# Fewer, wider tiles for the late modulation blocks in a hybrid decoder layer

## The chip, the cores and the metric

The kernel runs on one core of a Trainium2 chip. The metric is device time in microseconds (us), as the median of several executions. Before the change it is 1068.77 us, the median of 3 runs (1064.44 to 1072.26). The profile is of one further execution.

## What is computed

One layer of a decoder trunk works on 576 token rows: 512 of a prompt and 64 of eight samples. A condition vector `c` per prompt or sample (nine in all) is turned into six modulation vectors of 1024 each. Cut to what matters here, the reference is:

```
mod = silu(c) @ w_ada + b_ada                      # (9, 6144)
sh1, sc1, g1, sh2, sc2, g2 = split(mod, 6)
u = x * (1 + sc1) + sh1
z = u @ w_in                                       # pool, q, f, i, out gate, gate A, gate B
merged = sigmoid(z_ga) * (y_pool @ w_a) + sigmoid(z_gb) * (y_hgrn @ w_b)
x = layer_norm(ALPHA * x + g1 * (merged @ w_out))
h = x * (1 + sc2) + sh2
x = layer_norm(ALPHA * x + g2 * ((silu(h @ w_gate) * (h @ w_up)) @ w_down))
```

`w_ada` is 1024 by 6144, all of it float32: 24 MB. The first two of the six vectors (`sc1`, `sh1`) are needed at the start. The other four, 16 MB of weights, are needed only after the mixers, and the kernel computes them late, between the matmuls of the last gates. That late part is what the change is about.

## The kernel before, in words

The work is one program for five engines in these stages: the early modulation and `u`; `u @ w_in` with the two mixers, head by head; the eight gate pairs (`z_ga`, `z_gb`, 128 channels of each at a time); `y_pool @ w_a`; `y_hgrn @ w_b`; `merged @ w_out` with the first norm; the feed-forward; `w_down` with the second norm.

Large products are done by `fast` (line 210) as seven products of halves instead of eight. One product is twelve matmuls of 288 columns (`mm_q`, line 203, the matmuls have line 207), since each float32 operand is split in a high and a low part that are multiplied as hi*hi, hi*lo and lo*hi. `fast_w` (line 178) loads the two raw weight tiles of a product (512 KB each, three buffers `raw`, SyncE's queue) and makes the sums and splits of their quarters on POOL, ACT and DVE. `fast_u` (line 743) makes the weights of the next product ready and then runs the present one. `gate(m)` (line 786) is one such product for gate pair `m`. Its results go to the two tiles `SG[m]` (`sga`, `sgb`), first by an ACT copy (line 222), then by DVE additions (line 220). The seven products of a gate share four PSUM banks in turn.

`ada(blk)` (line 320) computes 256 columns of the modulation for the nine condition vectors. Its weights come as two tiles of four contraction blocks by 256 columns, 512 KB each with 1 KB of contiguous memory per row (`ada_load`, line 242, issue line 247). Each tile is multiplied by four float32 matmuls (line 328), one for each contraction block. They use 32 columns of the PE array each and write to different partitions of one PSUM bank (`tile_position`), so the four run side by side. I call these four matmuls a **batch**. Each float32 matmul shows as two instructions in the trace, so a batch is 8 instructions there. After two batches DVE copies the bank to `adaev` (line 332). For the two vectors that are wanted by channel (`SC2`, `SH2`), two small matmuls of nine columns (line 338, four instructions in the trace) add up the four partial sums and turn them, and DVE writes them to `mod` (line 340). For the two gates (`G1`, `G2`) the tile is stored in DRAM (`gada`, line 335), to be read and spread over the rows much later (`gate_bc`, line 889).

The sixteen late blocks are called in the loop over the gates (lines 802 to 805): three before each of the gates 2 to 5, two before 6 and 7. The pool `adap` holds three `ada` tiles and two `adaev` tiles. A scheduler in the compiler mixes the instructions of the blocks and the gates on each engine. Each engine, and SyncE's queue of loads, then runs its own instructions strictly in the order that is fixed when the program is built. A load that waits for a buffer holds back the loads behind it.

Two later places matter. `SG` tiles for gates 2 to 7 are taken at once (line 797) and stay until the product with `w_b` is merged. In the `w_out` stage (from line 990) SyncE's queue brings the eight `w_out` tiles (line 121), the rows of `x` for the residual (line 1000) and the first feed-forward weights (line 116), and DVE splits the weights (line 108) between its work for the norm (lines 926 to 948).

Of the kernel before, what the change touches and what calls it, by code (L numbers as in the profile page):

```python
# [9 lines left out]
ALU = mybir.AluOpType  # L10
PSUM = bass.MemoryType.PSUM

P = 128
D = 1024
KT = D // P
# [18 lines left out]
SH1, SC1, G1, SH2, SC2, G2 = 0, 8, 16, 24, 32, 40  # L34
# [3 lines left out]
C_ID, C_MP, C_MS, C_SEL, C_SP, C_SS, C_BM, C_RC, C_END = 0, 128, 256, 320, 330, 458, 522, 526, 552  # L38
# [27 lines left out]
def bcast(ap, n):  # L66

    return bass.AP(ap.tensor, ap.offset, list(ap.ap) + [[0, n]])


def trunk(tc, consts, x_prompt, x_sample, state_pool, state_hgrn, c_prompt, c_sample,
# [4 lines left out]
    pe, act, dve, pool, sp = nc.tensor, nc.scalar, nc.vector, nc.gpsimd, nc.sync  # L76
    pl = Pools(tc)
    t_ = pl.t
# [10 lines left out]
    s0, _s0 = pl.open("s0", "right")  # L89
# [3 lines left out]
    cst = t_(cp, [P, C_END], "cst")  # L93
# [3 lines left out]
    R_LB, R_NW, R_PS, R_BA, R_LG, R_LO, R_END = 0, 16, 24, 28, 76, 84, 92  # L97
# [35 lines left out]
    def prefetch(n):  # L133
        while len(ready) < n and seq:
            ready.append(load_w(seq.pop(0)))
# [31 lines left out]
    def split(hi, lo, src, eng=dve):  # L167
        act.copy(out=hi, in_=src)  # L168
        return eng.tensor_tensor(out=lo, in0=src, in1=hi.bitcast(F32), op=ALU.subtract)  # L169
# [72 lines left out]
    def ada_load(pl_, blk):  # L242

        raws = []
        for j in range(2):
            raw = t_(pl_, [P, 4, 256], "ada", bufs=8 if pl_ is s0 else 3)
            ada_last[0] = sp.dma_start(out=raw, in_=w_ada[0][j * 512:(j + 1) * 512, blk * 256:(blk + 1) * 256]
                         .rearrange("(k p) n -> p k n", p=P))
            raws.append(raw)
        return raws  # L250
# [56 lines left out]
    cpad = t_(ym, [P, KT, 32], "cpad")  # L307
    pool.memset(cpad, 0.0)
    pc = t_(psA, [P, 512], "t", bufs=2)
    for kt in range(KT):  # L310
        pe.transpose(out=pc[:, kt * 16:kt * 16 + 9], in_=sc_[:, kt * P:(kt + 1) * P], identity=ident[:9, :9])
    dve.tensor_copy(out=cpad[:, :, 0:9],
                    in_=pc[:, :P].rearrange("p (k c) -> p k c", c=16)[:, :, 0:9])

    mod = t_(cp, [P, 48, 9], "mod")

    dr, _dr = pl.open("gada", space=bass.MemoryType.DRAM)
    gada = {G1: t_(dr, [P, 4, 256], "gada1"), G2: t_(dr, [P, 4, 256], "gada2")}

    def ada(blk, pl_, psp, tag, raw=None):  # L320

        if raw is None:
            raw = ada_load(pl_, blk)
        ps = t_(psp, [P, 512], tag, bufs=2 if tag == "t" else 4)
        for st in range(2):
            for g in range(4):
                kt = st * 4 + g
                pe.matmul(out=ps[32 * g:32 * g + 32, :256], lhsT=cpad[:, kt, :], rhs=raw[st][:, g, :],  # L328
                          start=st == 0, stop=st == 1, tile_position=(0, 32 * g))
        m = blk * 2  # L330
        ev = t_(pl_, [P, 256], "adaev", bufs=2)
        dve.tensor_copy(out=ev, in_=ps[:, :256])
        if G1 <= m < SH2 or m >= G2:
            base = G1 if m < SH2 else G2
            sp.dma_start(out=gada[base][:, (m - base) // 2], in_=ev)
            return
        for j in range(2):
            pe.matmul(out=ps[:, 256 + 16 * j:256 + 16 * j + 9], lhsT=ev[:, j * P:(j + 1) * P],
                      rhs=cst[:, C_SEL:C_SEL + 9], start=True, stop=True)
        dve.tensor_tensor(out=mod[:, m:m + 2], in0=ps[:, 256:288].rearrange("p (j c) -> p j c", j=2)[:, :, 0:9],  # L340
                          in1=bcast(prow[:, R_BA + m:R_BA + m + 2], 9), op=ALU.add)

    prow = t_(cp, [P, R_END], "prow")
# [27 lines left out]
    for b in range(4):  # L371
        for kt in (2 * b, 2 * b + 1):
# [6 lines left out]
                              in1=bcast(sc[:, 1:9], LS), op=ALU.mult)  # L379
# [19 lines left out]
    def st_():  # L399
        return t_(psB, [P, 512], "s", bufs=4)  # L400
# [78 lines left out]
    psB, _psB = pl.open("psB", "right", space=PSUM)  # L479
# [146 lines left out]
    def vg():  # L626
        return t_(hp, [P, T], "v"), t_(hp, [P, T], "g", bufs=2)
# [95 lines left out]
    def hg4(h):  # L723
# [3 lines left out]
        for i in range(4):  # L727
# [5 lines left out]
        dve.scalar_tensor_tensor(out=YB[:, h, TP:T], in0=px[:, :TS], scalar=nw, in1=s["g"][:, TP:T],  # L733
                                 op0=ALU.mult, op1=ALU.mult)

    ada_todo = [SC2 // 2 + b for b in range(4)] + [SH2 // 2 + b for b in range(4)] + \
               [G1 // 2 + b for b in range(4)] + [G2 // 2 + b for b in range(4)]

    pairs = iter([(win(a + h), win(b + h)) for h in range(1, NH) for a, b in ((M_F, M_Q), (M_I, M_OG))] +
                 [(win(M_GA + m), win(M_GB + m)) for m in range(KT)])  # L740
# [10 lines left out]
    v, g = vg()  # L751
# [13 lines left out]
    psF, _psF = pl.open("psF", "left", space=PSUM)  # L765
    for h in range(1, NH):
# [4 lines left out]
        v, g = vg()  # L771
# [8 lines left out]
    def sg_open(n):  # L780
        p, cm = pl.open(f"sg{n}", "right")
        m0 = len(SG)
        SG.extend([[t_(p, [P, T], f"sg{x}{m}") for x in "ba"][::-1] for m in reversed(range(m0, m0 + n))][::-1])
        return cm

    def gate(m, mid=None):
        fast_u(*SG[m], mid)
        for x in SG[m]:
            act.activation(out=x, in_=x, func=AF.Sigmoid)

    _sga = sg_open(2)
# [2 lines left out]
    gate(1, lambda: hg3(NH - 1))  # L794
    hg4(NH - 1)
    pl.close(_hp)
    _sgb = sg_open(KT - 2)
    yah, _yah = pl.open("yahl", "right")
    YAH = t_(yah, [P, 4, T], "yah", F32R)
    YAL = t_(yah, [P, 4, T], "yal", F32R)  # L800
    adap, _adap = pl.open("ada", "right")
    for m in range(2, KT):
        for i in range(3 if m < 6 else 2):
            ada(ada_todo.pop(0), adap, psB, "s")
        gate(m)
        if m < 6:
            split(YAH[:, m - 2], YAL[:, m - 2], YA[:, m - 2])
        if m == KT - 1:
            seq += [("c", w_a[0], m, 4) for m in range(KT)]
            prefetch(2)  # L810
    pl.close(_adap)
    pl.close(_wu)
    pl.close(_tu)
    pl.close(_U)
# [4 lines left out]
    yt, _yt = pl.open("yt", "right")  # L819
    wy, _wy = pl.open("wy", "right")  # L820
# [17 lines left out]
    psF, _psF = pl.open("psF", "left", space=PSUM)  # L838
# [10 lines left out]
    for m in range(0, KT, 2):  # L849
# [9 lines left out]
        for i in range(2):  # L859
            a, b = SG[m + i]  # L860
            pool.tensor_tensor(out=b, in0=o[i], in1=b, op=ALU.mult)
            dve.tensor_tensor(out=a, in0=a, in1=b, op=ALU.add)
            split_act(MM[:, m + i], a)
    for c in (_wy, _yt, _yah, _sgb, _sga, _psF, _psB):
        pl.close(c)


# [13 lines left out]
    def bk():  # L881
        return t_(psC, [P, 512], "b", bufs=8)
# [6 lines left out]
    def gate_bc(pool_, mb):  # L889

        ga = t_(pool_, [P, D], "ga")
        act.dma_start(out=ga, in_=gada[mb].rearrange("p a b -> p (a b)"))
        act.dma_start(out=ga[R_BIAS:R_BIAS + 1], in_=b_ada[0:1, mb * P:mb * P + D])
        gp = t_(pool_, [P, D], "gp")
        gs = t_(pool_, [TS, D], "gs")
        for o, n, c in ((gp, P, C_SP), (gs, TS, C_SS)):
            for j in range(2):
                ps = bk()
                pe.matmul(out=ps[:n], lhsT=cst[:, c:c + n], rhs=ga[:, j * 512:(j + 1) * 512], start=True, stop=True)
                act.copy(out=o[:, j * 512:(j + 1) * 512], in_=ps[:n])  # L900
        return gp, gs
# [88 lines left out]
    ps = [bk() for i in range(5)]  # L990
    st = [t_(lp, [P, 2, 6], f"st{i}") for i in range(5)]
# [16 lines left out]
    for n, i in enumerate(order):  # L1008
        ps = bk()
# [36 lines left out]
    raw = load_raw(gate_up(1)[1])  # L1046
# [49 lines left out]
    g = [gemm_2(w) for w in w3[:2]]  # L1096
    swiglu(0, 1, *g)
    g = [gemm_2(w) for w in w3[2:]]
# [46 lines left out]
    st = [t_(dp, [P, 2, 6], f"st{i}") for i in range(5)]  # L1145
# [32 lines left out]
    ps = [bk() for i in range(5)]  # L1178
    for k in range(FT // 2):
# [3 lines left out]
        if 4 <= k < 9:  # L1183
            i = order[k - 4]
            n = P if i < 4 else TS
# [7 lines left out]
    ps = {i: bk() for i in order[:-1]}  # L1193
# [36 lines left out]
    for i in order[:-1]:  # L1230
        n = P if i < 4 else TS
# [7 lines left out]
    i = order[-1]  # L1239
    stl = t_(dp, [P, 3, 6], "stl")  # L1240
    act.copy(out=stl[:, 0], in_=st[i][:, 0])
    for h in range(2):
        for k in range(NL):
            down_part(FT // 2 - NL + k, *last[k], pe_[h], h)
        c = slice(512 + h * 256, 768 + h * 256)
# [59 lines left out]
```

## Time and profile before

| what | value |
|---|---|
| median of 3 runs | 1068.77 us (1064.44 to 1072.26) |
| the profiled execution, own time | 1066.02 us |
| its span, first to last instruction | 1063.9 us |
| around the span | 2.1 us |
| PE busy, share of the span | 984.7 us, 93% |
| VectorE (DVE) busy | 853.2 us, 80% |
| ScalarE (ACT) busy | 478.7 us, 45% |
| GpSimd (POOL) busy | 413.2 us, 39% |
| moved by DMA | 120.00 MB, mean 113 GB/s |
| mean granted TensorE clock | 0.977 of full speed |

PE is the matmul unit, PEld its weight loads. A busy time counts pipelined matmuls from their start to their modelled end, so consecutive matmuls overlap in it. Where a rate matters, the distance from one start to the next is read. In the chain of waits the profile follows the last instruction back through what released each step. Idle time before an instruction stands in brackets with what ended it.

### The profile page before, as it was taken

The page shows a single profiled execution, that of the slowest core. Times are in us where ns is not written, and L with a number is a line of the kernel's source. Part 1 is how long each engine was busy: PE and PEld are TensorE (multiplying, and loading weights), DVE is VectorE, ACT ScalarE, POOL GpSimd, SP SyncE. Part 2 cuts the span into 40 slices and gives each one's busy share as a digit, 9 for nine tenths or more (in the row PEclk, how much of TensorE's full clock was granted, in tenths as well). Part 3 has the DMA queues.
Part 4 walks back from the last instruction along what each step waited for, and adds up shares of the span by engine and source line. Part 5 has one row for each costly group of instructions (what it writes and reads, how often), then busy time and mean ns, then how long its engine had stood idle before and what let it go on. Part 6 is the DMA issues. An engine that isn't in the chain of part 4 may idle for free.

```text
span 1063.9 us, 17728 instructions
## 1 busy us (share of the span) xinstructions
PE 984.7 (93%) x6807; PEld 898.2 (84%) x6807; DVE 853.2 (80%) x1450; ACT 478.7 (45%) x861; POOL 413.2 (39%) x297
## 2 busy tenths in 40 slices
PE   5995889989999899999898998999999999999993
PEld 3885879989999897789897677999999999788882
DVE  3479998989989966436989498999999999957428
ACT  4342456665566464234333336444444434643312
POOL 1168675757666646365374011112212220000004
PEclk9997999999989999999999999999999999999997
DMA  9932142223323228893224810232332333432202
GB/s 258 293 90 66 41 121 81 83 83 102 100 72 93 87 78 255 274 282 101 89 71 130 256 40 21 60 93 87 99 95 85 99 91 110 139 119 80 80 20 89
DMA packets 170120, 120.00 MB, mean 113 GB/s; under 512 B 4286, under 2 KB 158938, under 8 KB 170028
## 3 DMA queue, kind: packets, MB, share of 16 engines
q1 hardware_dynamic: 168367, 114.25, 35.9%
q10 hardware_dynamic: 1668, 4.63, 1.3%
q8 instruction: 53, 0.87, 0.3%
q14 instruction: 32, 0.25, 0.1%
HBM read 110.57 MB, written 8.40 MB: 112 GB/s over the span
## 4 chain that ended last, share of the span: by engine, by line
PE 64%; DVE 21%; DMA 6%; issue 4%; POOL 2%; ACT 2%; SPq 0%; DVEq 0%; ACTq 0%; POOLq 0%
PE b L207 23%; PE f L207 16%; PE z L150 4%; DVE wlo L169 4%; PE b L1158 4%; PE b L1157 3%; PE b L1156 3%; DMA ada<-in_w_ada 2%; DMA raw<-in_w_in 2%; DMA raw<-in_w_up 2%; DVE tmp L581 1%; PE s L328 1%; DVE S L682 1%; PE b L1162 1%; PE b L1161 1%
## 5 line engine op out<-in xcount | busy, mean ns | idle before, releaser
L168 ACT CAST whi<-st 128x512 fp32r<-128x512 f32 x184 | 109.0, 618 | 105.4 <-POOL st L193 30.4
L169 DVE TENSOR_TENSOR wlo<-st,whi 128x512 fp32r<-128x512 f32 x140 | 127.7, 931 | 6.5 <-ACT whi L168 5.8
L187 POOL TENSOR_TENSOR st<-raw 128x512 f32<-128x512 f32 x36 | 56.8, 1578 | 134.9 <-DVE wlo L169 59.0
L207 PE MATMUL f<-uh,whi 128*128 128x288 f32 x352 | 106.7, 303 | 2.7 <-DVE tmp L220 1.6
L207 PE MATMUL f<-ul,whi 128*128 128x288 f32 x352 | 106.2, 302 | 0.0
L207 PE MATMUL f<-uh,wlo 128*128 128x288 f32 x352 | 105.8, 301 | 0.0
L108 DVE TENSOR_TENSOR wlo<-raw,whi 128x1024 fp32r<-128x1024 f32 (+1 forms) x46 | 55.1, 1197 | 34.8 <-ACT whi L107 34.5
L168 ACT CAST whi<-raw 128x1024 fp32r<-128x1024 f32 x46 | 48.3, 1049 | 76.5 <-PE f L207 32.6
L188 POOL TENSOR_TENSOR st<-st,raw 128x512 f32<-128x512 f32 x46 | 62.4, 1358 | 51.3 <-issue 49.6
L107 ACT CAST whi<-raw 128x1024 fp32r<-128x1024 f32 (+1 forms) x49 | 47.9, 978 | 63.0 <-PE b L1158 20.0
L1158 PE MATMUL b<-whi,hl 128*128 128x512 f32 (+1 forms) x198 | 72.6, 367 | 0.0
L1157 PE MATMUL b<-whi,hl 128*128 128x512 f32 (+1 forms) x198 | 72.5, 366 | 0.0
L207 PEld LDWEIGHTS f<-uh,whi 128*128 128x128 f32 x352 | 66.8, 190 | 6.6 <-DVE tmp L220 1.9
L1156 PE MATMUL b<-wlo,hl 128*128 128x512 f32 (+1 forms) x198 | 72.4, 365 | 0.0
L193 POOL TENSOR_TENSOR st<-raw,st 128x512 f32<-128x512 f32 x26 | 40.8, 1568 | 75.6 <-DVE wlo L169 71.3
L207 PEld LDWEIGHTS f<-ul,whi 128*128 128x128 f32 x352 | 66.8, 190 | 2.8 <-issue 2.5
L207 PEld LDWEIGHTS f<-uh,wlo 128*128 128x128 f32 x352 | 66.9, 190 | 2.2 <-issue 1.6
L1225 POOL TENSOR_TENSOR x<-x,lg 128x640 f32<-128x640 f32 (+2 forms) x4 | 5.9, 1465 | 160.0 <-ACT x L1216 160.0
L169 DVE TENSOR_TENSOR wlo<-raw,whi 128x1024 fp32r<-128x1024 f32 x46 | 65.0, 1413 | 3.2 <-ACT whi L168 3.1
L169 POOL TENSOR_TENSOR wlo<-st,whi 128x512 fp32r<-128x512 f32 x44 | 60.3, 1389 | 10.8 <-ACT whi L168 6.5
L207 PE MATMUL b<-bh,whi 128*128 128x288 f32 x184 | 54.5, 296 | 2.1 <-ACT bh L168 2.1
L207 PE MATMUL b<-bh,wlo 128*128 128x288 f32 x184 | 55.2, 300 | 0.0
(459 smaller groups left out, 3359.9 us busy)
## 6 DMA issues: line engine op xcount, KB each, us to landing
raw<-in_w_in SPq DMA_DIRECT2D x52, 512.0 KB
ada<-in_w_ada SPq DMA_DIRECT2D x48, 512.0 KB
raw<-in_w_gate SPq DMA_DIRECT2D x22, 512.0 KB
raw<-in_w_down SPq DMA_DIRECT2D x22, 512.0 KB
raw<-in_w_up SPq DMA_DIRECT2D x12, 512.0 KB
rawu<-in_w_up SPq DMA_DIRECT2D x10, 512.0 KB
s<-in_state_hgrn SPq DMA_DIRECT2D x8, 512.0 KB
out<-sn SPq DMA_DIRECT2D x8, 512.0 KB
```

The source lines that it names most:

```text
L107: act.copy(out=hi[:, :n], in_=raw[:, :n])
L108: eng.tensor_tensor(out=lo[:, :n], in0=raw[:, :n], in1=hi[:, :n].bitcast(F32), op=ALU.subtract)
L150: mm = pe.matmul(out=ps[:, GA0 + c0:GA0 + c1], lhsT=a[:, kt * P:(kt + 1) * P], rhs=x[:, kt, c0:c1], start=first and i == 0, stop=last and ...
L168: act.copy(out=hi, in_=src)
L169: return eng.tensor_tensor(out=lo, in0=src, in1=hi.bitcast(F32), op=ALU.subtract)
L187: pool.tensor_tensor(out=s1, in0=a21, in1=a22, op=ALU.add)
L188: pool.tensor_tensor(out=s2, in0=s1, in1=a11, op=ALU.subtract)
L193: eng.tensor_tensor(out=s4, in0=a12, in1=s2, op=ALU.subtract)
L207: pe.matmul(out=ps, lhsT=x[:, k * P:(k + 1) * P], rhs=y[:, k], start=first and k + i == 0, stop=last and k == 3 and i == 2)
L1156: pe.matmul(out=o, lhsT=xh, rhs=lo, start=first, stop=False)
L1157: pe.matmul(out=o, lhsT=xl, rhs=hi, start=False, stop=False)
L1158: return pe.matmul(out=o, lhsT=xh, rhs=hi, start=False, stop=last)
```

## The change

The late modulation gets its own function, `ada_late(m)`. It does 512 columns at a time from tiles of four contraction blocks by 512 columns, 1 MB each with 2 KB of contiguous memory per row. So there are 8 late blocks with two batches of 512 columns each (16 batches), where there were 16 blocks with two batches of 256 (32 batches). The copy to `adaev` takes 512 columns, and four small matmuls follow for `SC2` and `SH2`, into another PSUM bank. There are two `ada` buffers of 1 MB instead of three of 512 KB, and one `adaev` tile of 2 KB per partition instead of two of 1 KB. Gates 2 to 4 are each preceded by two late blocks, gates 5 and 6 by one, and gate 7 by none. The tiles of gate 7 are no longer taken with those of gates 2 to 6. They are taken when the pool of the modulation is closed, in memory that it held. The DRAM tiles `gada` lose their middle dimension. The early modulation keeps its size.

```diff
@@ ada_load
-            raw = t_(pl_, [P, 4, 256], "ada", bufs=8 if pl_ is s0 else 3)
+            raw = t_(pl_, [P, 4, 256], "ada", bufs=8)
@@
-    gada = {G1: t_(dr, [P, 4, 256], "gada1"), G2: t_(dr, [P, 4, 256], "gada2")}
+    gada = {G1: t_(dr, [P, D], "gada1"), G2: t_(dr, [P, D], "gada2")}
@@ ada
-        if G1 <= m < SH2 or m >= G2:
-            base = G1 if m < SH2 else G2
-            sp.dma_start(out=gada[base][:, (m - base) // 2], in_=ev)
-            return
@@
-    ada_todo = [SC2 // 2 + b for b in range(4)] + [SH2 // 2 + b for b in range(4)] + \
-               [G1 // 2 + b for b in range(4)] + [G2 // 2 + b for b in range(4)]
+    def ada_late(m, pl_):
+
+        ps = st_()
+        for st in range(2):
+            raw = t_(pl_, [P, 4, 512], "ada", bufs=2)
+            sp.dma_start(out=raw, in_=w_ada[0][st * 512:(st + 1) * 512, m * P:m * P + 512].rearrange("(k p) n -> p k n", p=P))
+            for g in range(4):
+                pe.matmul(out=ps[32 * g:32 * g + 32], lhsT=cpad[:, st * 4 + g, :], rhs=raw[:, g, :],
+                          start=st == 0, stop=st == 1, tile_position=(0, 32 * g))
+        ev = t_(pl_, [P, 512], "adaev")
+        dve.tensor_copy(out=ev, in_=ps)
+        if G1 <= m < SH2 or m >= G2:
+            base = G1 if m < SH2 else G2
+            sp.dma_start(out=gada[base][:, (m - base) * P:(m - base) * P + 512], in_=ev)
+            return
+        px = st_()
+        for j in range(4):
+            pe.matmul(out=px[:, 16 * j:16 * j + 9], lhsT=ev[:, j * P:(j + 1) * P],
+                      rhs=cst[:, C_SEL:C_SEL + 9], start=True, stop=True)
+        dve.tensor_tensor(out=mod[:, m:m + 4], in0=px[:, :64].rearrange("p (j c) -> p j c", j=4)[:, :, 0:9],
+                          in1=bcast(prow[:, R_BA + m:R_BA + m + 4], 9), op=ALU.add)
+
+    ada_todo = [SC2, SC2 + 4, SH2, SH2 + 4, G1, G1 + 4, G2, G2 + 4]
@@
-    _sgb = sg_open(KT - 2)
+    _sgb = sg_open(KT - 3)
...
     for m in range(2, KT):
-        for i in range(3 if m < 6 else 2):
-            ada(ada_todo.pop(0), adap, psB, "s")
+        for i in range(2 if m < 5 else 1 if m < KT - 1 else 0):
+            ada_late(ada_todo.pop(0), adap)
+        if m == KT - 1:
+            pl.close(_adap)
+            _sgc = sg_open(1)
         gate(m)
...
-    pl.close(_adap)
```

In the program as built, the matmuls of the late modulation stand between those of the gates on **PE**. Before, in gate 3 (`f_` a bank of the gate, `s_` one of the modulation; L328 a batch or half of one, L338 the small matmuls, L207 the gate):

```order
L328 MATMUL s_4688<-ada_4684,cpad_196 32x256 x2
L338 MATMUL s_4670<-cst_73,adaev_4679 128x9 x2
L328 MATMUL s_4688<-ada_4684,cpad_196 32x256 x2
L207 MATMUL f_4794<-t1l_833,whi_4537 128x288
L207 MATMUL f_4794<-t1h_832,wlo_4538 128x288
L207 MATMUL f_4808<-uh_81,whi_4539 128x288
L328 MATMUL s_4688<-ada_4686,cpad_196 32x256 x4
```

With the change, also in gate 3 (L739 a batch, L749 the small matmuls):

```order
L749 MATMUL s_4511<-cst_73,adaev_4509 128x9 x4
L739 MATMUL s_4652<-ada_4653,cpad_196 32x512 x4
L207 MATMUL f_4796<-uh_81,wlo_4526 128x288
L207 MATMUL f_4811<-t4h_836,hq_4545 128x288
L207 MATMUL f_4811<-t4l_837,hq_4545 128x288
L207 MATMUL f_4811<-t4h_836,lq_4546 128x288
```

The batches are twice as wide and half as many. Between two matmuls of the gates PE turns to the modulation at 30 places before and at 17 with the change, and no batch is cut in two any more. In the first gates a batch still follows after some 9 to 34 matmuls of a gate.

On **SyncE's queue** the loads of the modulation (`ada`) stand between those of the next gates (`raw`). Before, from the start of gate 2:

```order
L174 DMA raw_4533<-in_w_in 128x8x128
L247 DMA ada_4477<-in_w_ada 128x4x256
L247 DMA ada_4479<-in_w_ada 128x4x256
L247 DMA ada_4495<-in_w_ada 128x4x256
L174 DMA raw_4720<-in_w_in 128x8x128
L247 DMA ada_4497<-in_w_ada 128x4x256
L247 DMA ada_4513<-in_w_ada 128x4x256
L247 DMA ada_4515<-in_w_ada 128x4x256
L174 DMA raw_4722<-in_w_in 128x8x128
```

With the change, from the same place:

```order
L174 DMA raw_4519<-in_w_in 128x8x128
L737 DMA ada_4476<-in_w_ada 128x4x512
L737 DMA ada_4482<-in_w_ada 128x4x512
L174 DMA raw_4694<-in_w_in 128x8x128
L737 DMA ada_4497<-in_w_ada 128x4x512
L174 DMA raw_4696<-in_w_in 128x8x128
L737 DMA ada_4503<-in_w_ada 128x4x512
L174 DMA raw_4861<-in_w_in 128x8x128
```

Two loads of 1 MB lie ahead at the start instead of three of 512 KB, and the fourth of 1 MB stands behind the second `raw` load of gate 4.

The scheduler also moved something that the diff does not touch: on **SyncE's queue** in the `w_out` stage. Before (`x1` the rows for the residual):

```order
L174 DMA rawu_1298_7272<-in_w_up 128x8x128
L121 DMA raw_1198_6523<-in_w_out 128x2x512
L121 DMA raw_1201_6530<-in_w_out 128x2x512
L121 DMA raw_1204_6537<-in_w_out 128x2x512
L1000 DMA x1_1166_6431<-in_x_prompt 128x1024 x4
L1000 DMA x1_1166_6431<-in_x_sample 64x1024
L116 DMA raw_1207_6629<-in_w_gate 128x8x128
```

With the change:

```order
L174 DMA rawu_1270_7152<-in_w_up 128x8x128
L121 DMA raw_1170_6403<-in_w_out 128x2x512
L1019 DMA x1_1138_6311<-in_x_prompt 128x1024 x4
L1019 DMA x1_1138_6311<-in_x_sample 64x1024
L121 DMA raw_1173_6410<-in_w_out 128x2x512
L121 DMA raw_1176_6417<-in_w_out 128x2x512
L116 DMA raw_1179_6509<-in_w_gate 128x8x128
```

The five `x` loads now stand ahead of the last two `w_out` loads.

## Rows read from the trace of the kernel before

**Rows 1.** The page: busy time, share of the span and instructions.

```profile
PE 984.7 (93%) x6807; PEld 898.2 (84%) x6807; DVE 853.2 (80%) x1450; ACT 478.7 (45%) x861; POOL 413.2 (39%) x297
```

**Rows 2.** Busy us (instructions) of PE, PEld, DVE, ACT, POOL; clock; DMA share, GB/s.

```profile
407.40:497.00 89.60, 88.40 (x747) 71.11 (x746) 42.36 (x85) 30.70 (x49) 44.43 (x34) 1.00 0.81 249
497.00:510.00 13.00, 9.85 (x73) 9.41 (x72) 12.82 (x7) 6.91 (x9) 9.95 (x3) 1.00 0.14 40
...
596.00:600.00 4.00, 4.00 (x17) 2.81 (x17) 1.23 (x1) 2.49 (x4) 0.00 (x0) 1.00 1.04 403
```

**Rows 3.** The chain of waits, gates 2 to 7: start us, us, what.

```profile
407.54 0.57 PE s L328 x8
408.11 1.13 PE f L207 x7
...
415.88 6.21 DMA ada<-in_w_ada
...
443.20 5.49 DMA ada<-in_w_ada
...
454.63 1.43 PE s L328 x24
...
465.36 4.33 PE f L207 x31
469.70 1.00 PE s L328 x16
```

**Rows 4.** The timeline of PE: start, us, line, names, tile shape; idle before.

```profile
407.11 0.29 PE L207 MATMUL f<-t1l,whi 128*128 128x288 f32 x1
407.24 0.29 PE L207 MATMUL f<-t1h,wlo 128*128 128x288 f32 x1
...
427.32 0.63 PE L328 MATMUL s<-ada,cpad 128*32 128x256 f32 x4
427.88 0.61 PE L338 MATMUL s<-cst,adaev 128*128 128x9 f32 x4
428.42 0.62 PE L328 MATMUL s<-ada,cpad 128*32 128x256 f32 x4
428.98 0.40 PE L207 MATMUL f<-t1l,whi 128*128 128x288 f32 x1
...
592.86 2.96 PE L899 MATMUL b<-ga,cst 128*128 128x512 f32 x6 [0.60 <-DMA ga<-in_b_ada]
```

**Rows 5.** Groups of PE's instructions, 407.4 to 497: count, busy us, mean ns, idle before.

```profile
L328 PE MATMUL s<-ada,cpad 128*32 128x256 f32 x256 | 20.6, 389 | 1.2 <-DMA ada<-in_w_ada 1.1
...
L338 PE MATMUL s<-cst,adaev 128*128 128x9 f32 x32 | 4.6, 252 | 0.0
```

**Rows 6.** PE and PEld of line 207 alone in that stretch.

```profile
407.40:497.00 89.60, 68.36 (x458) 61.47 (x456) 1.00 0.81 249
```

**Rows 7.** Who SyncE's queue waited for, 407 to 497: total us, times, longest.

```profile
SPq L247 <- PE s L328: 17.4, 20, 1.9
```

**Rows 8.** Timelines of SyncE's queue and of DVE in the `w_out` stage.

```profile
591.23 2.75 SPq L1000 DMA_DIRECT2D x<-in_x_prompt  x4
...
595.29 3.76 SPq L116 DMA_DIRECT2D raw<-in_w_up  x1
...
607.30 1.22 DVE L108 TENSOR_TENSOR wlo<-raw,whi 128x1024 fp32r<-128x1024 f32 x1 [8.46 <-ACT whi L107]
609.11 1.22 DVE L108 TENSOR_TENSOR wlo<-raw,whi 128x1024 fp32r<-128x1024 f32 x1 [0.58 <-ACT whi L107]
610.33 1.37 DVE L926 TENSOR_TENSOR r<-b,gp 128x512 f32<-128x512 f32 x2
```

**Rows 9.** The chain of waits and PE's timeline, behind those loads.

```profile
595.29 12.64 DMA raw<-in_w_up
...
629.03 1.09 PE L967 MATMUL b<-cst,x 128*128 128x128 f32 x8 [1.37 <-DVE x L948]
```

More of the change, by code (lines that the diff above doesn't have):

```diff
@@ L323, in ada @@
             raw = ada_load(pl_, blk)
-        ps = t_(psp, [P, 512], tag, bufs=2 if tag == "t" else 4)
+        ps = t_(psp, [P, 512], tag, bufs=2)
         for st in range(2):
@@ L863, in trunk @@
             split_act(MM[:, m + i], a)
-    for c in (_wy, _yt, _yah, _sgb, _sga, _psF, _psB):
+    for c in (_wy, _yt, _sgc, _yah, _sgb, _sga, _psF, _psB):
         pl.close(c)
@@ L891, in gate_bc @@
         ga = t_(pool_, [P, D], "ga")
-        act.dma_start(out=ga, in_=gada[mb].rearrange("p a b -> p (a b)"))
+        act.dma_start(out=ga, in_=gada[mb])
         act.dma_start(out=ga[R_BIAS:R_BIAS + 1], in_=b_ada[0:1, mb * P:mb * P + D])
```

## Prediction

> **What bounds the kernel now.** I read the page first. PE is busy for 93% of the span [rows 1], so most changes must take work or waits from PE to show. Then the busy times by stretch, for the gates 2 to 7, in which the late modulation lies. From 407.4 to 497 us PE is busy 88.4 of 89.6 us, while DVE, ACT and POOL have half their time free or more and the DMA engines stand at 0.81 [rows 2]. So the stretch is PE's, with loads as the next limit. Right behind it, 497 to 510, DVE is busy 12.82 of 13 us and PE waits [rows 2]. That stretch starts from the results of gate 7 and should move with them as a whole. Then the chain of waits, which alternates between the gates (line 207) and the batches (line 328), with two loads of `ada` in it [rows 3]. Last, the order as built, for what the scheduler made of the change.
>
> A busy PE is not PE at its best, so I split these 89.6 us by starts. In the chain, 31 gate matmuls take 4.33 us and 7 take 1.13 us [rows 3]. The difference is 24 matmuls in 3.20 us, 0.133 us each, as their starts show (407.11 to 407.24 [rows 4]). Seven at that rate are 0.93, so resuming after a batch costs 0.20. The stretch holds 456 gate matmuls by the program (the trace has 458 records [rows 6]): 60.7 us. The other 28.9 us are the modulation and what surrounds it.
>
> **The change, part by part.**
>
> *Batches.* One batch alone takes 0.57 us on the chain, two in a row 1.00, three 1.43 [rows 3]. A further batch of 256 columns therefore streams in 0.43, and turning to the modulation costs 0.14. With the 0.20 for resuming, a visit costs 0.34. Before: 32 batches x 0.43 = 13.8; 30 visits x 0.34 = 10.2; waits of PE for `ada` 1.2 [rows 5]; what is left of 28.9 is 3.7 for the eight pairs of small matmuls, 0.46 a pair (one inside a batch took 0.54, from 427.88 to 428.42 [rows 4]).
>
> With the change: 16 batches of twice the columns stream the same 13.8. There are 17 visits: 5.8. Each of the four sets of small matmuls now has four: it costs between 0.46 (if a set costs what a pair did) and 0.92 (two pairs). They stay separate matmuls with their own weight loads, so I take 0.80: 3.2. Sum 22.8, which is 6.1 under 28.9 if nothing waits.
>
> The trace has no batch of 512 columns. From below it is 0.43 x 2 with one start; from above, two separate batches, 2 x 0.57 = 1.14, which adds 16 x 0.14 = 2.2. The nearest row with 512 float32 columns is line 899: six instructions, three matmuls, in 2.96 us, so 0.99 each with all starts and stops [rows 4]. Four side by side that cost 1.00 fit that, so I take the lower value.
>
> *Loads.* This is the part that can take the gain back. With two buffers, a load of 1 MB is issued when the batch two before it is done, and must land before PE comes to its own batch. Between the second and the twelfth batch in the new order stand 230 gate matmuls (30.6 us), ten batches (10.0), four sets of small ones (3.2) and resumes (about 2.8): 46.6 us, or 9.3 for two batches. Less one batch of 1.0, a load has 8.3 us. A load of 512 KB on the chain took 5.49 and 6.21 us to land [rows 3]. Another 512 KB adds 1.3 us at the 403 GB/s of 596 to 600 and 2.1 at this stretch's mean of 249 [rows 2]: 6.8 to 8.3 us. That just fits, but the batches are not evenly spaced. Where only 9 gate matmuls lie between two batches the later load is late, and one load stands behind a `raw` load that waits for POOL. I bound the waits from 0 to 3 us. SyncE's queue, which waited for PE's batches 20 times before [rows 7], still does, so they do not vanish. I take 1.6, somewhat above the 1.2 of now. The stretch is then 6.1 - 1.6 = **4.5 us** shorter.
>
> The Trainium skill, "DMA: Bandwidth & Descriptors", section "Bandwidth", puts a core's reads from HBM at about 358 GB/s at most, which speaks against any gain from the longer rows. Here a stretch of 4 us moved 403 GB/s [rows 2], so the trace does not agree. At 358 the added 512 KB would take an estimated 1.5 us instead of 1.3, and the sum would stay.
>
> *DVE, ACT, POOL.* Half as many copies of twice the width, half as many additions to `mod`, half as many stores: nothing on the path, since DVE is idle for half of the stretch [rows 2]. One `adaev` tile instead of two: a copy waits until the small matmuls or the store of the block before have read it. Blocks are over 7 us apart, and a store is smaller than the loads that landed in 5.49 to 6.21 [rows 3].
>
> *Gate 7's tiles.* ACT's first copy of gate 7 now waits until the last `adaev` is stored. The last batch stands after the first matmul of gate 6's last product. Behind it come 23 gate matmuls, 3.1 us, to the end of gate 7's first product. PE can go on for three more products in the other banks, 3 x 12 x 0.133 = 4.8 us. So the store has 7.9 us. Copy and landing need about 0.8 + 6.2 = 7.0, with the slowest load as the bound. I cost it at nothing. If it took longer, each us over 7.9 would stop PE. Queued behind the copy on ACT are only splits for `w_a`, which have the same cover.
>
> *The moved `x` loads.* In the `w_out` stage the five `x` loads (issued from 591.23 before [rows 8]) now stand ahead of the last two `w_out` loads. These have buffers to wait for, so the `x` loads use a gap, and 2.25 MB no longer lie in front of the `w_gate` and `w_up` loads. Before, a `w_up` load issued at 595.29 took 12.64 us and stands on the chain [rows 9]. The two splits behind it sit on DVE at 607.30 and 609.11, each 1.22, directly ahead of the norm's first work at 610.33 [rows 8], and PE later waits 1.37 for that DVE work [rows 9]. Landing earlier takes the second split (1.22) from that path. The gain lies between 0 and the 1.37 of that wait, plus a 0.60 wait at line 899 [rows 4] that the new order fills with other matmuls. A later landing of the last two `w_out` tiles could cost as much, but they are wanted only after the first half. I take **1.1**, near the split, less a little for two norm steps that move behind others on DVE.
>
> *Sum.* 4.5 + 1.1 = 5.6 us. The profiled execution took 1066.02 us (span 1063.9 and 2.1 around it) and would take 1060.4. It lies 2.7 under the median of the runs shown, 1068.77, from which the same sum gives 1063.2. I forecast 1063.0 as a median.
>
> **Rivals.**
>
> *A. The wide batches save little.* Each batch of 512 columns costs 1.14 (2.2 back), the small sets cost 0.92 (0.5 back), waits reach 3 (1.4 back) and the moved loads bring nothing (1.1). 5.6 - 5.2 leaves 0.4: 1068.4. For it: no row shows such a batch beside gates. Against it: the clean 0.43 steps for batches in a row.
>
> *B. Slower: the two buffers make PE wait in every batch.* Two loads are never far ahead, and for ten batches each pair takes landing plus 1.0. At a landing of 9.7 us a pair takes 10.7 where 9.3 stand in the sum. That is 1.4 x 5 = 7.0 lost, 1.6 of it already counted, so the 5.6 is gone. At 12 us it is 13 - 9.3 = 3.7 x 5 = 18.5: 16.9 beyond the sum, 11.3 over now, 1080. For it: `raw` loads stand between in the same queue, and another load took 12.64 us when the queue was full [rows 9]. Against it: 5.49 to 6.21 in this very stretch [rows 3].
>
> *C. Much more is won.* No waits in the stretch (1.6 more), sets at 0.46 (1.4), the whole 1.37 and 0.60 at the moved loads (0.9), and DVE's full stretch from 497 on starts with its `w_a` weights ready, so that part of PE's 3.15 us there goes (say 2): 5.6 + 5.9 = 11.5, 1057. For it: every one of these is a wait that rows show. Against it: all must come at once.
>
> *D. The change doesn't do what it says.* Gate 7's tiles come so late that PE stands still: at a landing of 10 us the store needs 10.8, 2.9 over its cover, and the gain shrinks to 2.7: 1066. It needs a store slower than any load of the stretch.
>
> **How the numbers follow.** Forecast 0.60, A 0.15, B 0.09, C 0.10, D 0.06. A measurement of this kernel can tell about 1% (10.7 us) from no change. Faster by more than that comes from C and the luckiest of the forecast: 0.12. Slower by more comes from B's far end: 0.07. The rest, 0.81, is within 1%. The likeliest case's own terms reach from 3 to 9 us of gain, 1060 to 1066, and three runs of the kernel before lie 8 us apart. The range 1055 to 1071 holds all but part of B and the ends of C.
>
> **What would show it.** On PE: batches of line 739 alone at about 1.00 us from start to the next gate matmul; resumes of 0.20; sets of line 749 at 0.8; waits for `ada` of 1 to 3 us in all, most of them in gates 3 and 4; the time from the start of gate 2 to the first `w_a` matmul shorter by 4 to 5. On ACT: the copy to `sga7` not ended by a store, or with PE not idle. In the `w_out` stage: the `w_gate` and `w_up` loads landed well before the first half ends, and the norm's first step not behind a split. Wrong would be loads of 1 MB that land later than 8.3 us as a rule, batches near 1.14, or a PE wait in gate 7.

## The result and the profile after

| | before | after |
|---|---|---|
| median | 1066.40 us of 15 runs (1062.43 to 1072.26) | 1058.51 us of 15 runs (1054.87 to 1065.18) |
| ratio | | 0.9928, 95% interval 0.9906 to 0.9949 |
| the profiled execution, and its span | 1066.02 and 1063.9 us | 1061.09 and 1059.3 us |

The changed kernel is 0.7% faster. The interval is a gain of 5.4 to 10.0 us; the working of the prediction came to 5.6.

First the stage of gates 2 to 7, by the windows: busy us (and instructions) of PE, PEld, DVE, ACT and POOL, then clock, DMA share and GB/s. Before, it ran from 407.40 to 497 [rows 2].

```profile
407.40:492.00 84.60, 83.15 (x619) 67.30 (x618) 40.09 (x73) 30.92 (x49) 44.30 (x34) 1.00 0.80 260
492.00:505.00 13.00, 9.88 (x74) 9.44 (x72) 12.78 (x8) 6.93 (x9) 9.96 (x3) 1.00 0.14 42
```

The stage is 5 us shorter, PE is still busy for all but 1.45 us of it, and the DVE stretch behind it only moved. The chain of waits shows what PE does there (start, us, what), to be held against [rows 3].

```profile
413.37 3.50 PE f L207 x25
416.87 0.79 PE s L749 x8
417.66 1.00 PE s L739 x8
418.65 3.50 PE f L207 x25
422.15 1.05 PE s L739 x8
...
448.83 1.04 PE s L739 x8
449.89 8.54 DMA ada<-in_w_ada
458.47 1.11 PE s L739 x8
459.60 8.93 DMA ada<-in_w_ada
468.57 1.06 PE s L739 x8
```

A batch of 512 columns takes 0.99 to 1.11 us, mostly 1.00. A set of four small matmuls takes 0.79. 25 gate matmuls in 3.50 us are 25 x 0.133 = 3.32 and a resume of 0.18. Two loads of 1 MB stand on the chain, and the groups of PE in this stretch say what they cost.

```profile
L739 PE MATMUL s<-ada,cpad 128*32 128x512 f32 x128 | 17.0, 604 | 1.4 <-DMA ada<-in_w_ada 1.3
...
L749 PE MATMUL s<-cst,adaev 128*128 128x9 f32 x32 | 3.8, 246 | 0.0
```

PE idles 1.4 us ahead of these batches, 1.3 of it for `ada`, where it idled 1.2, 1.1 of it for `ada` [rows 5]. The copy to gate 7's new tile, from ACT's timeline:

```profile
483.04 0.40 ACT L222 COPY sga<-f 128x288 f32<-128x288 f32 x1 [0.84 <-PE f L207]
```

Its wait was ended by PE's own product, not by the store. Gate 7's tiles cost nothing here.

Second, the `w_out` stage: SyncE's queue, the chain, DVE's timeline and PE's, which answer to [rows 8, 9] and the last row of [rows 4]. `ga` is the tile that `gate_bc` reads back from `gada`, on ACT's queue. When it has landed, the row of `b_ada` (the bias row) is written over one of its rows, and then the `ga` matmuls can start.

```profile
579.76 1.92 SPq L1019 DMA_DIRECT2D x<-in_x_prompt  x4
```

```profile
580.39 8.93 DMA ga<-gada
589.34 4.57 DMA ga<-in_b_ada
594.04 2.96 PE b L918 x6
```

```profile
603.75 1.23 DVE L108 TENSOR_TENSOR wlo<-raw,whi 128x1024 fp32r<-128x1024 f32 x1 [2.27 <-ACT whi L107]
606.00 1.37 DVE L945 TENSOR_TENSOR r<-b,gp 128x512 f32<-128x512 f32 x2 [1.02 <-PE b L930]
```

```profile
594.04 2.96 PE L918 MATMUL b<-ga,cst 128*128 128x512 f32 x6 [1.00 <-DMA ga<-in_b_ada]
...
624.70 1.09 PE L986 MATMUL b<-cst,x 128*128 128x128 f32 x8 [1.37 <-DVE x L967]
```

The `x` loads are early now, and the second split no longer stands directly ahead of the norm: DVE idles 1.02 us and PE's product ends that. Yet the norm starts 114.0 us behind the first `w_a` matmul (491.99 to 606.00), where it was 113.4 (496.95 to 610.33), and PE waits the same 1.37 behind it. This part gave nothing that shows.

### The profile page after: what moved, and what is told of

Same layout as the page of the kernel before. It is cut to its first block, busy times and chain, and to the rows that moved or that the text cites. A ratio compares the mean times of both kernels' runs of the same rounds, so it can differ in the third digit from the quotient of the medians.

```text
span 1059.3 us, 17409 instructions
## 1 busy us (share of the span) xinstructions
PE 977.0 (92%) x6679; PEld 892.3 (84%) x6679; DVE 854.3 (81%) x1438; ACT 479.1 (45%) x861; POOL 412.1 (39%) x297
## 4 chain that ended last, share of the span: by engine, by line
PE 62%; DVE 22%; DMA 6%; issue 5%; POOL 2%; ACT 2%; SPq 0%; DVEq 0%; ACTq 0%; POOLq 0%
PE b L207 23%; PE f L207 13%; DVE wlo L169 4%; PE z L150 4%; PE b L1177 4%; PE b L1176 4%; PE b L1175 3%; DMA ada<-in_w_ada 3%; PE s L739 1%; DVE tmp L577 1%; DVE S L678 1%; DVE g L220 1%; PE b L1181 1%; PE b L1180 1%; DMA ga<-gada 1%
## 5 line engine op out<-in xcount | busy, mean ns | idle before, releaser
L207 PE MATMUL f<-uh,whi 128*128 128x288 f32 x352 | 105.9, 301 | 2.7 <-DVE tmp L220 1.6
L207 PE MATMUL f<-uh,wlo 128*128 128x288 f32 x352 | 105.5, 300 | 0.0
L207 PE MATMUL f<-ul,whi 128*128 128x288 f32 x352 | 105.2, 299 | 0.0
L207 PEld LDWEIGHTS f<-uh,whi 128*128 128x128 f32 x352 | 66.4, 189 | 7.1 <-issue 2.5
L207 PEld LDWEIGHTS f<-uh,wlo 128*128 128x128 f32 x352 | 66.6, 189 | 3.1 <-issue 2.5
L207 PEld LDWEIGHTS f<-ul,whi 128*128 128x128 f32 x352 | 66.4, 189 | 1.1 <-issue 0.8
L207 PE MATMUL b<-bh,whi 128*128 128x288 f32 x184 | 55.2, 300 | 2.1 <-ACT bh L168 2.1
L207 PE MATMUL b<-bh,wlo 128*128 128x288 f32 x184 | 55.6, 303 | 0.0
```

Source lines behind the costliest of these rows:

```text
L207: pe.matmul(out=ps, lhsT=x[:, k * P:(k + 1) * P], rhs=y[:, k], start=first and k + i == 0, stop=last and k == 3 and i == 2)
```

## Experiments

Single executions scatter, so one yardstick serves all profiles: the stretch from the first matmul `f<-t1h,whi` of gate 2, ahead of the first batch, to the first `w_a` matmul. Its row in the windows gives its length and, as PE's busy time, what PE did in it without the waits. The second stretch goes from the last `w_a` matmul to the norm's first step on DVE; from it PE's largest wait at or near the `ga` matmuls is taken off. All in us:

| run | gate 2 reached | gates 2 to 7 | PE busy there | w_a to norm | wait | less wait |
|---|---|---|---|---|---|---|
| before | 405.78 | 91.17 | 89.97 | 82.91 | 0.60 | 82.3 |
| before_again | 402.63 | 93.38 | 90.15 | 83.63 | 1.68 | 82.0 |
| after | 405.82 | 86.17 | 84.73 | 83.39 | 1.00 | 82.4 |
| after_again | 404.30 | 84.46 | 84.46 | 85.42 | 2.42 | 83.0 |
| narrow_mm | 402.02 | 85.89 | 85.22 | 83.55 | 0.95 | 82.6 |
| short_rows | 403.83 | 87.39 | 84.57 | 85.18 | 2.76 | 82.4 |
| x_late | 401.34 | 84.84 | 84.64 | 84.40 | 1.96 | 82.4 |
| ga_two | 404.15 | 84.58 | 84.58 | 84.72 | 2.14 | 82.6 |
| ga_two_x_late | 402.27 | 86.52 | 84.59 | 85.72 | 3.31 | 82.4 |

**The two kernels again.** Both unaltered.

> The changed kernel once more, unaltered, to see how far one profiled execution of it differs from another. Theory (the gain is the 5.0 us that gates 2 to 7 became shorter, all of it on PE): about 5 us, ratio 0.9955 to 0.995, and gates 2 to 7 again as long as before to within 0.3 us. Rival (something outside these gates gives a further 3 us): ratio near 0.9925, and a second place in the program where the starts move by 2 us or more against the kernel before.

> The kernel before, unaltered, for a second profile of it. Theory (how early gate 2 is reached scatters from profile to profile, 401.4 to 405.8 us over the versions so far, whatever stands behind it): this profile reaches it somewhere in 401 to 406 us, and takes 90 to 92 us from there to the first w_a matmul and 566 to 568 us from there to the end. Rival (the change gains time ahead of gate 2 too): gate 2 is reached at 405.5 us or later again.

after_again: 1059.14 us, ratio 0.9928 (0.9904 to 0.9951). before_again: 1065.42 us, ratio 0.9989 (0.9969 to 1.0010). The rows of the stage, after_again and then before_again:

```profile
404.30:488.76 84.46, 84.46 (x631) 68.85 (x629) 41.29 (x74) 31.88 (x50) 45.81 (x35) 1.00 0.81 267
```

```profile
402.60:496.00 93.40, 90.15 (x758) 72.59 (x757) 43.92 (x86) 31.65 (x50) 46.02 (x35) 1.00 0.80 246
...
L328 PE MATMUL s<-ada,cpad 128*32 128x256 f32 x256 | 20.6, 389 | 3.3 <-DMA ada<-in_w_ada 3.3
```

PE's busy time repeats to 0.3 us, and the waits don't: 0 and 1.4 us for `ada` in two executions of the changed kernel, 1.2 and 3.3 in two of the kernel before. So after_again's stage is 1.7 us shorter than the first profile's, where it was expected within 0.3 of it. Its ratio is the rival's, but the second place that the rival asked for does not show: `w_a` to norm is no shorter, and gate 2 is reached at 402.63 in before_again, within the range of the other profiles. The stage took before_again 93.4 us, above the 90 to 92 expected, and the 3.3 us of waits are why.

**narrow_mm: visits or width?** The tile of 512 columns stays, but is multiplied in two batches of 256 back to back.

```diff
-            for g in range(4):
-                pe.matmul(out=ps[32 * g:32 * g + 32], ..., rhs=raw[:, g, :], ...)
+            for c in range(2):
+                for g in range(4):
+                    pe.matmul(out=ps[c][32 * g:32 * g + 32, :256], ..., rhs=raw[:, g, c * 256:c * 256 + 256], ...)
...
```

> The changed kernel with each tile of 512 columns multiplied as two batches of 256 columns right behind each other, in two PSUM banks, with two copies to adaev. Loads, buffers and visits are those of the change. Theory (streaming 0.43 us a batch of 256 is not saved, turning and resuming at 17 places instead of 30 is): a pair takes 1.00 as one wide batch does, so gates 2 to 7 change by less than 1 us and the time by less than 0.1%. Rival (it is the width of the matmuls that saves): a pair takes 1.14 or more, 16 x 0.14 = 2.2 us or more come back.

1058.16 us, ratio 0.9927 (0.9902 to 0.9951). On its chain, two batches of 256 columns take what one of 512 does:

```profile
405.38 1.00 PE s L740 x16
408.45 1.00 PE s L740 x16
```

PE's busy time is 85.22, about 0.6 above the changed kernel's and 4.8 below that of before. PE turns to the modulation at 19 places in this trace and not at 17, because one set of small matmuls more stands apart from the batches and another is cut in two. Two visits at the 0.32 that one_load shows below would be the whole 0.6. So the width of the matmul is worth at most 0.6 us and perhaps nothing. What is left is the number of times that PE turns from the gates to the modulation and back, and the small matmuls, whose busy time fell from 4.6 [rows 5] to 3.8.

**short_rows: length of the rows.** Each tile comes in two transfers with 1 KB per row.

```diff
-            sp.dma_start(out=raw, in_=w_ada[0][..., m * P:m * P + 512]...)
+            for c in (0, 256):
+                sp.dma_start(out=raw[:, :, c:c + 256], in_=w_ada[0][..., m * P + c:m * P + c + 256]...)
```

> The changed kernel with each tile of 512 columns loaded by two transfers of 256 columns, so contiguous rows of 1 KB as before the change, in the same buffers. Theory (loads have nearly enough time, and the row length matters little): the waits of PE for ada grow from 1.4 us by 0 to 2, the time by at most 2 us. Rival (the longer rows carry the gain, since loads are the next limit): waits grow by 4 us or more and most of the 5 us is gone.

1059.41 us, ratio 0.9936 (0.9911 to 0.9961); PE's busy time 84.57. PE waited 2.8 us for `ada`, the most of the profiles with these tiles, but before_again has 3.3 and the ratio can't be told from the changed kernel's. The gain does not hang on longer rows.

**one_load: no loads, fewer visits.** The tiles of the first late block serve all eight; 14 MB of loads and the right modulation values are left out.

```diff
-            raw = t_(pl_, [P, 4, 512], "ada", bufs=2)
-            sp.dma_start(out=raw, ...)
+            if m == SC2:
+                raw = t_(pl_, [P, 4, 512], "ada", bufs=2)
+                sp.dma_start(out=raw, ...)
+                late_raw.append(raw)
+            raw = late_raw[st]
```

> Left out: the late weight tiles of all blocks but the first (14 MB of loads); every late batch multiplies the same two tiles, so the instructions on PE stay. Theory (the loads of 1 MB cost only the waits that the records name, 0 to 2.8 us over the profiles so far, 1.0 in the mean): no wait for ada, the way from gate 2 to the first w_a matmul 84.5 us, the whole time 0 to 2 us below the changed kernel's, 1057 to 1059 us. Rival (the full queues slow more than those waits, other loads or the stage of w_a too): 4 us or more below, 1054 us or less.

1055.69 us, ratio 0.9894 (0.9871 to 0.9918): 3 us below the changed kernel, more than the theory said and less than the rival. The stage row and the chain:

```profile
405.24:486.96 81.72, 81.72 (x631) 69.48 (x630) 40.81 (x73) 31.60 (x50) 46.27 (x35) 1.00 0.31 97
```

```profile
417.07 1.85 PE s L744 x16
423.22 1.85 PE s L744 x16
429.40 1.85 PE s L744 x16
435.56 3.57 PE s L744 x32
```

Without waits for loads the scheduler put batches next to each other: the sixteen stand in 8 visits instead of 17. A second batch in a visit costs 0.85, four cost 3.57, so each streams in 0.86 and turning costs 0.14. PE's busy time fell by 2.9 against 84.6, or 0.32 for each of the nine visits less, where the prediction had 0.34. The loads are gone in this kernel too, but a lone batch takes 1.00 on its chain as with them, so this is the price of a visit.

**no_late: the whole late part.** Batches, small matmuls and loads are left out, so the last four modulation vectors are constants.

```diff
-        ps = st_()
-        for st in range(2):
...
-        dve.tensor_copy(out=ev, in_=ps)
+        dve.memset(ev, 0.125)
...
-        px = st_()
...
+        dve.tensor_copy(out=mod[:, m:m + 4], in_=bcast(prow[:, R_BA + m:R_BA + m + 4], 9))
```

> Left out: the sixteen late batches, their small matmuls and the loads of their weights; the copies, the stores of the gates' modulation and everything behind them stay, fed with a constant. Theory (the late modulation costs what its parts cost on PE): after it the gates 2 to 7 hold only their own 456 matmuls, 60.7 us, so the way from gate 2 to the first w_a matmul is 16 x 1.00 + 16 x 0.20 + 4 x 0.79 + the waits of about 1 us = 23 to 24 us shorter, and the whole time about 1035 us. Rival (something else would hold the gates at nearly the present pace, POOL with 44 us of work or the loads of w_f and w_up): under 15 us shorter, above 1043 us.

1040.29 us, ratio 0.9741 (0.9715 to 0.9767), 18 us below the changed kernel.

```profile
404.86:468.72 63.86, 63.15 (x470) 62.28 (x469) 44.32 (x68) 31.38 (x50) 48.31 (x35) 1.00 0.35 103
```

The stage is 22.3 us shorter than in the profile of after, a little less than the 23 to 24 expected, and PE waits only 0.7 us in it. The rival is out: nothing else holds the gates. The 1035 us of the theory was missed: the profiled execution took 1035.67, the other three 1040.13 to 1040.78. The late modulation costs PE 89.97 - 63.15 = 26.8 us before and about 21.4 after. The sums of the prediction, without waits, had 27.7 and 22.8 for these, 0.9 and 1.4 too much.

**x_late: the moved loads.** The `x` loads go back behind the last `w_out` load.

```diff
...
-                sp.dma_start(out=X1[...], in_=x_prompt[...] if i < 4 else xs_flat)
+            with tc.issue_after(last_ld[0].ins):
+                for i in range(5):
+                    sp.dma_start(out=X1[...], in_=x_prompt[...] if i < 4 else xs_flat)
```

> The changed kernel with the five x loads of the w_out stage put back behind the last w_out load in SyncE's queue, as before the change. Theory (the moved loads brought nothing, since the gate rows on ACT's queue then land later and PE waits 1.0 us for them instead of 0.6): the w_out stage gets 0 to 1 us shorter, the time stays within 1 us of the changed kernel. Rival (the prediction's term: the moved loads gain 1.1): 1 us longer.

1058.44 us, ratio 0.9924 (0.9898 to 0.9951): the same as with early loads, though an interval of some 3 us either way could not show 1.1. DVE's timeline ahead of its norm can, and there PE sets the norm's start too:

```profile
599.80 1.23 DVE L108 TENSOR_TENSOR wlo<-raw,whi 128x1024 fp32r<-128x1024 f32 x1 [0.50 <-ACT whi L107]
602.26 1.37 DVE L947 TENSOR_TENSOR r<-b,gp 128x512 f32<-128x512 f32 x2 [1.24 <-PE b L932]
```

What the early loads do change is the load of `ga`. ACT's queue issues it, and the bias row when it has landed; before, and then in x_late:

```profile
585.05 0.36 ACTq L892 DMA_DIRECT2D ga<-gada  x1
589.71 0.24 ACTq L893 DMA_DIRECT2D ga<-in_b_ada  x1
```

```profile
575.52 0.36 ACTq L913 DMA_DIRECT2D ga<-gada  x1
580.38 0.24 ACTq L914 DMA_DIRECT2D ga<-in_b_ada  x1
```

That is 4.66 and 4.86 us, against the 8.93 of the profile of after. So with the `x` loads early the load of `ga` takes nearly twice as long.

**ga_split, ga_two, ga_two_x_late: the wait for `ga`.** If PE sets the norm, its wait for the bias row of `ga` should be worth money. Three kernels tried to take that row out of the serial chain of two loads. The first loads `ga` in three pieces that don't overlap: the bias row, the 118 rows below it and the nine rows above it.

```diff
-        act.dma_start(out=ga, in_=gada[mb])
-        act.dma_start(out=ga[R_BIAS:R_BIAS + 1], in_=b_ada[...])
+        act.dma_start(out=ga[R_BIAS:R_BIAS + 1], in_=b_ada[...])
+        act.dma_start(out=ga[R_BIAS + 1:], in_=gada[mb][R_BIAS + 1:])
+        act.dma_start(out=ga[:R_BIAS], in_=gada[mb][:R_BIAS])
```

> The tile ga is loaded in three pieces that don't overlap (the bias row, the rows below and those above it), where now the bias row is written over the loaded tile and so issued when that has landed. Theory (behind the moved x loads, PE and no longer the split on DVE sets the norm, and PE waits there for the bias row): the wait of 0.95 to 2.76 us at the ga matmuls goes, and the time is 1 to 2.5 us below the changed kernel's, 1056 to 1058 us. Rival (the tile itself lands as late as the bias row does, or the split is late again): within 0.5 us of the changed kernel.

1079.32 us, ratio 1.0119 (1.0088 to 1.0150): 20 us slower than the changed kernel, which neither theory had. From ACT's queue, the chain, PE's timeline and the windows:

```profile
573.50 0.25 ACTq L912 DMA_DIRECT2D ga<-gada  x1
573.78 0.40 ACTq L913 DMA_DIRECT2D ga<-gada  x1
```

```profile
573.78 21.75 DMA ga<-gada
```

```profile
595.66 1.19 PE L919 MATMUL b<-ga,cst 128*128 128x512 f32 x1 [14.51 <-DMA ga<-gada]
```

```profile
586.00:595.00 9.00, 0.00 (x0) 0.00 (x0) 0.00 (x0) 0.00 (x0) 0.00 (x0) 0.50 0.13 51
```

PE waits 14.51 us for `ga`. By its start, the piece that ends the wait is the last one issued, the nine rows (L913); the 118 rows were issued just ahead of it (L912). From 586 to 595 us no engine but the DMA works, at 0.13 of the sixteen DMA engines. That is two of them. What they move is the piece of 118 rows, since the nine rows have only 36 KB and this queue still moved 0.34 MB from 585 to 595 us. The nine rows landed no earlier:

```profile
q10 hardware_dynamic: 87, 0.34, 8.7%
```

The Trainium skill, "DMA: Bandwidth & Descriptors", section "Why a DMA increments its semaphore by 16 and not by 1", says that a transfer is spread over the largest number of engines, at most 16, that divides its outer dimension. For 118 rows that is 2, and the share of 0.13 agrees.

```diff
-        act.dma_start(out=ga, in_=gada[mb])
+        act.dma_start(out=ga[:32], in_=gada[mb][:32])
+        act.dma_start(out=ga[32:], in_=gada[mb][32:])
```

> The tile ga is loaded in two pieces, rows 0 to 31 and rows 32 to 127 (96 rows, not the odd 118 of the run ga_split), and the bias row is written when the small piece has landed. Theory (the moved x loads stretch the load of ga, 4.4 to 4.7 us from its issue to the issue of the bias row before and 7.1 to 9.0 us with them, so that PE waits 0.95 to 2.76 us for the bias row, which hides what the earlier x loads gain): the bias row no longer comes last, the wait falls under 0.5 us, the way from the end of w_a to the norm is 82.4 to 82.8 us instead of 83.4 to 85.4, the time 1 to 2 us below the changed kernel's. Rival (any further piece costs as the pieces of ga_split did): a wait for ga of 3 us or more, the time above the changed kernel's.

> The same two pieces, with the x loads put back behind the last w_out load. Theory: the wait of 1.96 us for the bias row goes here too, the split on DVE is then what stands ahead of the norm, as in the kernel before, and the way from the end of w_a to the norm is 82.8 to 83.5 us; the time within 1 us of the run ga_two, 0 to 1.5 us below the changed kernel's. Rival (the x loads' place decides nothing because PE sets the norm in both): the same way as in ga_two to 0.2 us, and PE, not DVE, ahead of the norm.

ga_two: 1059.09 us, ratio 0.9938 (0.9915 to 0.9961). ga_two_x_late: 1060.61 us, ratio 0.9940 (0.9918 to 0.9962). No gain, so that theory fell as well. PE's timeline of ga_two:

```profile
586.99 2.96 PE L919 MATMUL b<-ga,cst 128*128 128x512 f32 x6 [2.14 <-DMA ga<-in_b_ada]
```

The pieces of 32 and 96 rows bring no trouble, and the `ga` matmuls start 69.2 us behind the last of `w_a` (517.83 to 586.99) where it was 71.4 in the profile of after (522.61 to 594.04). But their place in PE's order moved ahead as well (52 matmuls of `w_out` stand before them in this trace, 68 in that of after), so PE came there sooner and waited 2.14. ga_two_x_late waits at the same place, there 3.31 for DVE. A change of one load also moved the order that the scheduler builds around it, and the wait came back. A version that takes it away with PE's order kept was not run, so what it is worth stays open.

## Why the prediction was right, and where it was not

**The stage, forecast 4.5 us shorter: right.** The two profiles shown differ by 5.0, and PE's busy time by 89.97 - 84.73 = 5.2, over all profiles by 5.2 to 5.7 (before 89.97 and 90.15 against 84.46 to 84.73 with the wide batches). By terms:

- Batch of 512 columns at 1.00: measured 1.00, of which one_load shows 0.86 to be streaming, as for two batches of 256, and 0.14 turning. The upper bound of 1.14 is out.
- Visit at 0.34: one_load gives 0.32. Thirteen visits less are 4.2 to 4.4 us, the largest part of the gain, and narrow_mm shows that it comes without wide matmuls.
- Set of small matmuls at 0.80: 0.79.
- Gate 7's tiles at nothing: shown by ACT's copy, which waits for PE.
- The sum without waits: 27.7 to 22.8, or 4.9 less, where 26.8 to 21.4, or 5.4 less, was measured. Both ends were too high, by 0.9 and 1.4, and that this cancels for the most part is luck.

**Waits for `ada`, forecast 1.6: right in size, wrong in place and in working.** The profile of after has 1.4. But the loads that PE waited for landed at 458 and 468 us, in gates 5 and 6, not in gates 3 and 4. They took 8.54 and 8.93 us, above the 6.8 to 8.3 of the estimate, so its margin was gone in the worst places. Rival B did not follow, since only two of the sixteen loads stand on the chain: by the landing events in the trace the sixteen took 5.4 to 8.9 us, and four of them more than 8.3. And the single number meant little: 0 to 2.8 us came out for the same tiles, 1.2 and 3.3 before. The mean of the two profiles of before, 2.25, is above that of the seven others of the table, (1.4 + 0 + 0.7 + 2.8 + 0.2 + 0 + 1.9) / 7 = 1.0 (the stage less PE's busy time). This may be part of the rest between 5.2 and what the medians show, 7.9. Two profiles against seven don't prove it, and the waits at `ga` in the table go the other way: 0.60 and 1.68 before, 0.95 to 3.31 in the seven.

**The moved `x` loads, forecast 1.1: the failed step.** The working took the second split's 1.22 as the price, because it sits "directly ahead of the norm's first work". (Only that one of the two splits is behind the late `w_up` load, which landed at 595.29 + 12.64 = 607.93, when the first had begun.) What was not read is when PE would have released the norm anyway. The last product for that tile, in PE's timeline of the kernel before:

```profile
609.90 0.39 PE L911 MATMUL b<-whi,mm 128*128 128x512 f32 x1
```

And the same product in the changed kernel:

```profile
605.57 0.39 PE L930 MATMUL b<-whi,mm 128*128 128x512 f32 x1
```

In the changed kernel DVE is idle, and the norm starts at 606.00, 0.43 us behind the start of this product. Before, it starts at 610.33, also 0.43 us behind 609.90. So PE set the norm before as well; the split ended just then and held it for nothing, not for 1.22. In before_again the split does hold it. PE, then DVE:

```profile
609.02 0.39 PE L911 MATMUL b<-whi,mm 128*128 128x512 f32 x1
```

```profile
608.86 1.23 DVE L108 TENSOR_TENSOR wlo<-raw,whi 128x1024 fp32r<-128x1024 f32 x1 [0.53 <-ACT whi L107]
610.00 1.28 DVE L926 TENSOR_TENSOR r<-b,gp 128x512 f32<-128x512 f32 x2
```

There PE allowed the norm at 609.02 + 0.43 = 609.45, and it starts 0.55 us later. So the split was worth 0 and 0.55 us in two profiles. The 0.60 us wait that the new order was to fill became 1.00: 68 matmuls of `w_out` stand ahead of it in the trace of after, 44 in that of before, but `ga` landed late, beside the `x` loads. The table says the same: less the wait near `ga`, the way from `w_a` to the norm is 82.0 to 83.0 us in all nine profiles, wherever the `x` loads stand, and with the wait it is longer with the new tiles (83.39 to 85.72) than before (82.91 and 83.63).

**The sum and the median.** 5.6 was forecast, with 1.1 of it in the wrong place; the two profiles differ by 4.9 in their own times and the medians by 7.9. The forecast of 1063.0 was 4.5 us high. 2.4 of that are the start, since 1068.77 was a median of 3 runs and 15 gave 1066.40. The other 2.1 are inside the scatter that the table shows at three places: when gate 2 is reached (401.3 to 405.8), the waits for `ada`, and the wait at `ga`. Rivals A and D are out by the terms above, though A was right that the moved loads bring nothing, and B's long waits did not come. C's time of 1057 came close, but not by its mechanism: the 1.37 stayed and the sets cost 0.79.

## What to carry to other kernels

Where PE alternates between two kinds of matmul, count the visits: here one cost about 0.32 us on top of the streaming, and doing twice as much per visit was worth more than wider matmuls or longer rows. An instruction that stands directly ahead of another on an engine is not yet its price: look at when the other's inputs were ready, and count only the difference. And repeat a profile before a term of one or two microseconds is believed, since the waits for `ada` differed by 1.4 and 2.1 us between two executions of one kernel.

## What was not expected of the hardware

A load of 118 rows ran on 0.13 of the DMA engines. It was issued at 573.50, and `ga` was complete at 595.53, some 22 us later, where the full 128 rows took 8.93 in the profile of after and pieces of 32 and 96 rows did no harm. While PE stood idle for it, the granted clock fell to 0.50, its lower level of 1.2 GHz, and the first matmul behind it took 1.19 us. Transfers with 1 KB rows instead of 2 KB did not show in PE's time. They did in the DMA engines', which were busy for 0.84 of the stage instead of 0.80. For nearly the same bytes that is about 0.84 x 87.37 = 73.4 us against 0.80 x 86.18 = 68.9, in short_rows and then in after (and 0.80 x 93.40 = 74.7 in before_again, whose tiles have 1 KB rows too):

```profile
403.83:491.20 87.37, 84.57 (x630) 68.87 (x629) 41.40 (x73) 31.94 (x50) 46.44 (x35) 1.00 0.84 261
```

```profile
405.82:492.00 86.18, 84.73 (x631) 68.88 (x630) 41.66 (x74) 31.98 (x50) 45.80 (x35) 1.00 0.80 263
```
